# Values of one head and gates of the preceding head projected as one 512-column panel

## The chip, the core and the metric

The kernel runs on one core of a Trainium2 chip. The metric is the device time of one execution, in microseconds; lower is better. Engines are called by the names of the profile: PE is TensorE, ACT ScalarE, DVE VectorE, POOL GpSimd, SP SyncE (here a queue of DMA issues).

## The reference

One inference step of a layer with two groups of eight heads, for a prompt of 1024 tokens and for 8 x 16 = 128 sample tokens:

```
h = rms_norm(x, norm_pre)
q_sb, k_sb, v_sb, gate_sb, q_r, k_r, v_r, gate_r = split(h @ w_in)      # 8 kinds x 8 heads x 128
o_sb = stick_breaking(q_sb, k_sb, v_sb)        # per 128-query block, causal; samples over a cache of 1024
o_r  = retention(rope(q_r), rope(k_r), v_r)    # chunks of 64, a 128x128 state per head
y_sb = rms_norm_per_head(o_sb) * gain * silu(gate_sb)
y_r  = rms_norm_per_head(o_r)  * gain * silu(gate_r)
out  = concat(y_sb, y_r) @ w_out
x   += rms_norm(out, norm_post)
```

All is float32. The new keys and values and the retention states are outputs too.

## The kernel before

**Products.** A float32 product is done as three matmuls on float32r operands: high x high, high x low, low x high, where `split` (L165) makes the high part on ScalarE and the low part on VectorE. The tokens go in two groups: group 0 is four prompt tiles of 128 and the sample tile (640 tokens), group 1 the other four prompt tiles (512). The normalised tokens of a group lie in SBUF, transposed (model dimension on partitions), as high and low parts; the weights of `w_in` come from memory in blocks of 256 KB through tile `wr` (five buffers) and are split into `wh` and `wl` (four buffers). The 2048 rows of a weight are 16 k-tiles.

**Column panels** (`project`, L401; `products`, L382). For six of the eight kinds a panel is one head's 128 columns: the weights are the stationary operand, the tokens move, 256 + 384 columns in group 0, 512 in group 1. The result is transposed (head dimension on partitions, tokens along the row), which queries, keys and, before, gates need. One panel is 48 steps of k and term, each followed by a `tick` (L228). A panel uses one bank of tag `acc0` and, in group 0, one of `acc1`; there are two of each.

**Row panels** (`project_rows`, L424). Values are needed with tokens on partitions. Here the tokens are stationary, a tile of 128 at a time, and the weights of a pair of heads move, 256 columns. One panel serves heads h and h+1 of one kind; two token tiles share a bank. The values of retention are `rv`, those of attention `vn`. ScalarE copies them out with each token's inverse root (`root_of`).

**Gates** (`gate`, L475). A gate panel is a column panel; its result is scaled (VectorE), goes through a sigmoid (ScalarE) and is multiplied by it (VectorE): silu, transposed. The finish of a branch (`Out.finish`, L705) normalises the head's outputs (tokens on partitions), writes them to memory and reads them back in 32-blocks that a VectorE transpose completes (`turn_out`, `turn_in`: the "turn"), then multiplies gain, outputs and gate and stores the result to `s_y`, from which the output projection reads.

**Order.** The order is written by hand. The panels of a head come as query, key and gate of retention, then query and key of attention, the values of a pair at every second head, the gate of attention; retention's values of the next pair follow an odd head. Around the last heads the order differs (L1183 to L1196). The work of attention and retention lies between the matmuls of the panels: each is a generator (`Job`, L222) that yields a number of ticks to wait; `tick` advances the clock by one and runs one step of one job that is due. The constants `D_...` (L30 to L60) are these waits. `drain` (L241) ticks without products until a job is done: retention's job of the preceding head is drained behind the next head's query panel of retention, attention's job and the sample's `decode` behind the next query panel of attention. `tied` and `pin` keep some instructions from being placed ahead of the last product. What is written goes through a scheduler, which makes the order of each engine's queue from it.

Beside these jobs, in group 1, a job `sums` makes sums of blocks of `w_out` (40 items) for an output projection in seven products, and `residuals` writes the input rows to the outputs. Banks of PSUM: four for panels, two for score tiles (`score_tile`, L688; a third one in group 1), one each for `psa` and `psd`.

## Time and profile before

| | |
|---|---|
| time, median of 3 runs | 2277.81 us (2276.71 to 2277.94) |
| the profiled execution, first to last instruction | 2278.3 us |
| matmuls | 14306 |
| granted TensorE clock, mean | 0.996 |
| moved by DMA | 463.13 MB, mean 203 GB/s |

Busy times of engines overlap. A group's row gives line, engine, operation, output <- inputs, shape and count, then its busy time in us and the mean ns of one, then the idle time of the engine just before it and what ended most of it. The chain of work that ended last is followed back from the last instruction; in order of time it gives start, us and what. A row of waits gives in total, times, longest. A DMA issue gives count, KB each, median us to landing. Matmuls are pipelined, so the mean duration of one is longer than the distance from one to the next.

### The profile page before, as it was taken

To read this page: it belongs to the slowest core of one execution; us is meant where nothing else is said; L and a number is where in the kernel's file an instruction comes from. 1 tells how busy PE (TensorE), PEld (TensorE's weight loads), DVE (VectorE), ACT (ScalarE), POOL (GpSimd) and SP (SyncE) were. 2 spreads that over 40 slices of the span, in tenths; PEclk is the share of its full clock that TensorE was granted. 3 is DMA by queue.
4 is the path that set the end of the run, shared out by engine and by line. 5 is a ranking of instruction groups with operands and counts; after the bars stand their busy time and mean duration, and the time that the engine had idled before them with its cause. 6 is when DMAs were issued, how large, how long until landed. Compare 5 with 4: busy or idle time off the path is not lost.

```text
span 2278.3 us, 38962 instructions
## 1 busy us (share of the span) xinstructions
PE 2241.5 (98%) x14306; PEld 2023.3 (89%) x14306; DVE 1263.7 (55%) x2606; ACT 919.8 (40%) x1951; POOL 340.6 (15%) x577
## 2 busy tenths in 40 slices
PE   8999999999999999999999999999999999999998
PEld 8999999999999999999887989888888988788886
DVE  5435544454545454456556665766665667555567
ACT  6433333333333333335343334343343445435363
POOL 0012120301202030121111111120212212000020
PEclk9999999999999999999999999999999999999999
DMA  8747656675656657578778888878787758865596
GB/s 284 233 153 199 196 159 194 176 220 159 182 194 181 194 165 209 177 200 269 193 225 207 220 220 235 206 226 238 220 231 213 216 165 190 252 205 182 146 222 172
DMA packets 440832, 463.13 MB, mean 203 GB/s; under 512 B 182336, under 2 KB 302144, under 8 KB 440128
## 3 DMA queue, kind: packets, MB, share of 16 engines
q1 hardware_dynamic: 318400, 300.16, 46.5%
q0 software_dynamic: 28720, 78.41, 12.3%
q10 hardware_dynamic: 93520, 82.07, 11.4%
q8 instruction: 112, 1.84, 0.3%
q14 instruction: 80, 0.66, 0.1%
HBM read 359.58 MB, written 110.36 MB: 206 GB/s over the span
## 4 chain that ended last, share of the span: by engine, by line
PE 88%; DMA 5%; DVE 3%; issue 2%; ACT 2%; SPq 0%; POOL 0%; DVEq 0%; ACTq 0%; POOLq 0%
PE acc L387 46%; PE accn L446 17%; PE a L1213 5%; PE a L1214 5%; PE a L1210 5%; PE pa L783 3%; PE z L753 2%; PE pd L886 1%; PE zc L822 1%; DMA ro<-s_rk 1%; DMA s_rk<-rk 1%; PE pa L931 1%; PE pS L946 1%; DVE kp L682 1%; DMA wr<-w_cols 1%
## 5 line engine op out<-in xcount | busy, mean ns | idle before, releaser
L387 PE MATMUL acc<-mh,wh 128*128 128x256 f32 (+2 forms) x2304 | 667.4, 341 | 6.9 <-ACT wh L167 6.9
L387 PE MATMUL acc<-ml,wh 128*128 128x256 f32 (+2 forms) x2304 | 662.7, 340 | 0.2
L387 PE MATMUL acc<-mh,wl 128*128 128x256 f32 (+2 forms) x2304 | 659.8, 338 | 0.0
L168 DVE TENSOR_TENSOR wl<-wr,wh 128x512 fp32r<-128x512 f32 x504 | 345.9, 689 | 428.0 <-ACT wh L167 401.7
L167 ACT ACTIVATE wh<-wr 128x512 fp32r<-128x512 f32 x504 | 317.3, 631 | 641.2 <-PE acc L387 347.2
L387 PEld LDWEIGHTS acc<-mh,wh 128*128 128x128 f32 x2304 | 421.4, 189 | 39.2 <-ACT wh L167 6.9
L387 PEld LDWEIGHTS acc<-ml,wh 128*128 128x128 f32 x2304 | 422.9, 189 | 32.1 <-issue 3.3
L387 PEld LDWEIGHTS acc<-mh,wl 128*128 128x128 f32 x2304 | 425.5, 189 | 27.8 <-DVE wl L168 0.2
L446 PE MATMUL accn<-whn,mh 128*128 128x256 f32 x1152 | 328.1, 285 | 0.0
L446 PE MATMUL accn<-wln,mh 128*128 128x256 f32 x1152 | 325.8, 283 | 0.8 <-DVE wln L168 0.8
L446 PE MATMUL accn<-whn,ml 128*128 128x256 f32 x1152 | 325.7, 283 | 0.0
L446 PEld LDWEIGHTS accn<-whn,mh 128*128 128x128 f32 x1152 | 220.7, 192 | 2.7 <-issue 0.8
L446 PEld LDWEIGHTS accn<-wln,mh 128*128 128x128 f32 x1152 | 220.7, 192 | 1.8 <-DVE wln L168 1.0
L446 PEld LDWEIGHTS accn<-whn,ml 128*128 128x128 f32 x1152 | 220.7, 192 | 0.0
L167 ACT ACTIVATE whn<-wrn 128x512 fp32r<-128x512 f32 x128 | 80.5, 632 | 183.2 <-PE acc L387 74.2
L168 DVE TENSOR_TENSOR wln<-wrn,whn 128x512 fp32r<-128x512 f32 x128 | 87.6, 687 | 117.4 <-ACT whn L167 113.5
L646 POOL DMA_DIRECT2D be<-s_be x128 | 94.1, 741 | 149.5 <-DMA s_be<-be 126.4
L682 DVE TENSOR_TENSOR_SCAN kp<-kp 128x1152 f32<-128x1152 f32 (+4 forms) x40 | 82.7, 2067 | 45.7 <-POOL kp L671 29.1
L809 POOL DMA_DIRECT2D kcT<-cache_k x64 | 34.6, 545 | 442.2 <-PE pd L886 268.2
L1210 PE MATMUL a<-wh,mh 128*128 128x512 f32 x240 | 94.0, 392 | 1.8 <-ACT wh L167 1.8
L671 POOL TENSOR_SCALAR_AFFINE_SELECT kb<-kb 128x128 f32<-128x128 f32 x64 | 29.8, 474 | 433.2 <-ACT kb L665 430.9
L1213 PE MATMUL a<-wl,mh 128*128 128x512 f32 x240 | 94.3, 393 | 0.2 <-DVE wl L168 0.2
(272 smaller groups left out, 2968.7 us busy)
## 6 DMA issues: line engine op xcount, KB each, us to landing
wr<-w_cols SPq DMA_DIRECT2D x384, 256.0 KB, 4.4
wrn<-w_rows SPq DMA_DIRECT2D x128, 256.0 KB, 3.7
kcT<-cache_k POOLq DMA_DIRECT2D x64, 512.0 KB, 8.2
vc<-cache_v SPq DMA_DIRECT2D x64, 512.0 KB, 6.0
wr<-s_b SPq DMA_DIRECT2D x80, 256.0 KB, 4.1
br<-w_out SPq DMA_DIRECT2D x64, 256.0 KB, 4.9
s_b<-br ACTq DMA_DIRECT2D x32, 512.0 KB, 5.5
wr<-w_out SPq DMA_DIRECT2D x48, 256.0 KB, 3.7
```

The costliest lines, as they stand in the source:

```text
L167: nc.scalar.activation(hi, src, AF.Copy),
L168: nc.vector.tensor_tensor(lo, src, hi.bitcast(F32), ALU.subtract),
L387: last = nc.tensor.matmul(a[:, :m], lhs[:, j, :], rhs[w][:, j, o : o + m], start=(w == 0 and j == 0 and n == 0), stop=(w == KT // WQ - 1 a ...
L446: anchor[0] = nc.tensor.matmul(a, lhs[q][:, jj, ts], rhs[:, j, :], start=(w == 0 and j == 0 and n == 0 and t % 2 == 0), stop=(w == KT // 2 ...
L646: q.dma_start(raw[32 * i : 32 * i + 32, :].rearrange("p (k a) -> p k a", a=32), s[:, :, 32 * i : 32 * i + 32].rearrange("k (j b) a -> b (k ...
L682: nc.vector.tensor_tensor_scan(rev, rev, rev, 1.0, ALU.mult, ALU.bypass)
L753: nc.tensor.matmul(z[:, :c], q2[a][:, i * P : (i + 1) * P], k2[b][:, s : s + c], start=(m == 0), stop=(m == 2),)
L783: nc.tensor.matmul(po[:, :P], at[:, j, :], vn[:, j, :], start=(j == 0), stop=(j == t))
L809: ready.append((kc, nc.gpsimd.dma_start(kc, cache_k[h, m // 4, m % 4])))
L1210: ins = nc.tensor.matmul(a, hi[k][:, ts], wh, start=first, stop=False)
L1213: nc.tensor.matmul(a, hi[k][:, ts], wl, start=False, stop=False)
L1214: anchor[0] = nc.tensor.matmul(a, lo[k][:, ts], wh, start=False, stop=last)
```

## The change

The gates are made with tokens on partitions, like the values, and both kinds of gate of head h-1 share one panel with both kinds of value of head h: four blocks of 128 columns, so 512 columns move past each token tile. The first values panel and the last gates panel of each group have 256 columns. Queries and keys stay column panels. The first query panel of attention takes the place of the first gate panel in the opening.

The middle panel takes four accumulation banks, one for each token tile, and in group 0 a score bank for the fifth. It ticks twice for each token tile and k-tile, 0.75 each. At its end each tile is copied out (values) and goes through a sigmoid that reads PSUM with the token's inverse root as scale, and a fused multiply (gates). The finish multiplies outputs, inverse root and gate before the turn, a token tile at a time; behind the turn only the gain is left. A branch's finish waits until the gates of its head are there, which is behind the next head's middle panel.

Values are in a tile of two buffers, `vv`, by head and group; in group 1 the four old value tiles come back from memory into a tile of their own, `vo`, ahead of the job. The waits for values in attention fall away. The host lays the weights out for the new panels.

```
-COLS = (0, 1, 3, 4, 5, 7)
-ROWS = (2, 6)
+COLS = (0, 1, 4, 5)
...
-    def tick():
-        clock[0] += 1
+    def tick(by=1):
+        clock[0] += by
...
-    def project_rows(g, mov, col, dst, off, loads=None, roots_first=None):
+    def project_rows(g, mov, part, banks, out, loads=None, first=True, ready=None):
...
+        nt, width = len(g["tiles"]), part.shape[-1]
+        per = 512 // width
+        share = 1 if per == 2 else 0.75
+        for w in range(KT // per):
+            wr = wp.tile([P, per, width], F32, name="wrn", tag="wr", bufs=5)
+            nc.sync.dma_start(wr, part[:, per * w : per * (w + 1), :])
...
+            wh = wp.tile([P, per, width], F32R, name="whn", tag="wh")
+            wl = wp.tile([P, per, width], F32R, name="wln", tag="wl")
             split(wh, wl, wr)
-            for j in range(2):
+            for j in range(per):
+                k = per * w + j
                 for t in range(nt):
...
                     for n, (lhs, rhs) in enumerate(((hi, wh), (hi, wl), (lo, wh))):
                         anchor[0] = nc.tensor.matmul(
-                            a,
+                            banks[t],
                             lhs[q][:, jj, ts],
                             rhs[:, j, :],
...
                         )
-                    tick()
+                        if per == 1 and n == 1:
+                            tick(share)
+                    tick(share)
...
         for t in range(nt):
+            out(t, banks[t], root_of[:, tiles_before(g) + t : tiles_before(g) + t + 1])
...
-        def gate(acc, tag):
...
+        def value_rows(key):
+            values[key] = ep.tile([P, 5, 2, P], F32, name="vv", tag="vv", bufs=2)
+
+            def out(t, a, root):
+                nc.scalar.activation(values[key][:, t].rearrange("p j d -> p (j d)"), a, AF.Copy, scale=root)
+
+            return out
+
+        def gate_rows(key):
+            made = ep.tile([P, 5, 2, P], F32, name="gg", tag="gg")
+
+            def out(t, a, root):
+                s = ep.tile([P, 2 * P], F32, name="sg", tag="sg")
+                nc.scalar.activation(s, a, AF.Sigmoid, scale=root)
+                nc.vector.scalar_tensor_tensor(
+                    made[:, t].rearrange("p j d -> p (j d)"), a, root, s, ALU.mult, ALU.mult
+                )
+                gated[key] = made
+
+            return out
+
+        def first_values(g, mov, loads=None, ready=None):
+            project_rows(g, mov, w_val, half_banks(g), value_rows((phase[0], 0)), loads, True, ready)
+
+        def last_gates(g, mov, loads=None):
+            project_rows(g, mov, w_gate, half_banks(g), gate_rows((phase[0], H - 1)), loads, False)
+
+        def between(g, mov, h):
+            banks = [accp.tile([P, 512], F32, name=f"accm{t}", tag=f"acc{t % 2}") for t in range(4)]
+            if SAMPLE in g["tiles"]:
+                banks.append(score_tile("accm4"))
+            v, u = value_rows((phase[0], h)), gate_rows((phase[0], h - 1))
+
+            def out(t, a, root):
+                v(t, a[:, : 2 * P], root)
+                u(t, a[:, 2 * P :], root)
+
+            project_rows(g, mov, w_mid[h - 1], banks, out)
...
-            first = *first, pair["r"][:, :, 0, :], dict(rg=gate(project(g0, mov, col(7, 0)), "rg"))
+            first.append(project(g0, mov, col(0, 0)))
...
-            def finish(self, b, h, gT, oT, dst):
+            def finish(self, b, gi, h, at, oT, dst):
                 rs = inv_rms(op, self.ssq, P, "o")
-                nc.vector.tensor_tensor(
-                    self.o, self.o, rs.unsqueeze(2).to_broadcast([P, self.nt, P]), ALU.mult
-                )
+                for i in range(self.nt):
+                    nc.vector.scalar_tensor_tensor(
+                        self.o[:, i, :], self.o[:, i, :], rs[:, i : i + 1], gated[gi, h][:, at + i, b, :], ALU.mult, ALU.mult
+                    )
...
                 tied(nc.vector.transpose(oT[:, :n], flat))
-                nc.vector.scalar_tensor_tensor(
-                    gT[:, :n], oT[:, :n], gains[:, b, h : h + 1], gT[:, :n], ALU.mult, ALU.mult
-                )
-                nc.scalar.dma_start(dst, gT[:, : self.nt * P])
+                nc.vector.tensor_scalar(flat, oT[:, :n], gains[:, b, h : h + 1], None, ALU.mult)
+                nc.scalar.dma_start(dst, flat)
...
-            while "rg" not in rest:
+            while (gi, h) not in gated:
                 yield 3
-            yield from out.finish(1, h, rest["rg"], rk, s_y[gi][H + h])
+            yield from out.finish(1, gi, h, 0, rk, s_y[gi][H + h])
...
+                    if gi == 1:
+                        vo = ip.tile([P, 4, P], F32, name="vo", tag="vo", bufs=1)
+                        nc.sync.dma_start(vo, s_v[h])
+                        rest["vn"] = [vo[:, i, :] for i in range(4)] + new
                     sb_job = Job(sb_branch(gi, g, h, out, q2, k2, kT, rest), D_NAT[phase[0]])
...
                 if (gi, h) == (0, 0):
-                    order = ret_start, attention, gates
-                elif gi == 0 or h < H - 3:
-                    order = ret_queries, ret_keys, ret_gate, attention, gates
-                elif h == H - 3:
-                    order = ret_queries, ret_keys, attention, ret_gate, gates
+                    order = ret_start, attention
+                elif gi == 0 or h < H - 2:
+                    order = rows, ret_queries, ret_keys, attention
                 elif h == H - 2:
-                    order = ret_queries, attention, ret_keys, ret_gate, gates
+                    order = rows, ret_queries, attention, ret_keys
                 else:
-                    order = attention, ret_queries, ret_keys, ret_gate, gates
+                    order = rows, attention, ret_queries, ret_keys
...
+            after = [[], []]
+            loads = first_left() if gi else load_moving(after, 0, NB_TOK, from_h)
+            if gi == 0:
+                next(loads)
+            last_gates(g, mov, loads)
...
+        "w_val": beside(w[2, 0], w[6, 0]),
+        "w_mid": a(np.stack([beside(w[2, h], w[6, h], w[3, h - 1], w[7, h - 1]) for h in range(1, H)])),
+        "w_gate": beside(w[3, H - 1], w[7, H - 1]),
```

Here `rows` runs the middle panel of its head (`between`), or at the first head of group 1 the first values panel.

158 lines of the change are left out of this document (48 added, 110 removed).

## The prediction

> **What bounds the kernel now.** I read the page first: busy shares, the forty slices, the chain of work that ended last.
>
> ```profile
> span 2278.3 us, 38962 instructions
> PE 2241.5 (98%) x14306; PEld 2023.3 (89%) x14306; DVE 1263.7 (55%) x2606; ACT 919.8 (40%) x1951; POOL 340.6 (15%) x577
> ...
> PE   8999999999999999999999999999999999999998
> ...
> PE 88%; DMA 5%; DVE 3%; issue 2%; ACT 2%; SPq 0%; POOL 0%; DVEq 0%; ACTq 0%; POOLq 0%
> ```
>
> TensorE is busy in every slice and carries 88% of the chain. No other engine passes 55%. Then the waits of PE, to see what is not pure streaming:
>
> ```profile
> PE pa L783 <- DVE kp L743: 8.1, 7, 2.4
> PE acc L387 <- ACT wh L167: 6.9, 1, 6.9
> PE pb L557 <- DVE dg L555: 3.1, 1, 3.1
> ```
>
> These are the three largest, and only the first recurs. So the end moves almost one for one with what the stream of matmuls costs, and there is little idle time to win back. Now the groups of instructions with the shapes kept apart (count, then busy us and mean ns of one):
>
> ```profile
> L446 PE MATMUL accn<-whn,mh 128*128 128x256 f32 x1152 | 328.1, 285 | 0.0
> ...
> L387 PE MATMUL acc<-mh,wl 128*128 128x512 f32 x768 | 303.5, 395 | 0.0
> ...
> L387 PE MATMUL acc<-mh,wh 128*128 128x384 f32 x768 | 260.5, 339 | 0.0
> ...
> L387 PE MATMUL acc<-mh,wh 128*128 128x256 f32 x768 | 222.5, 290 | 6.9 <-ACT wh L167 6.9
> ...
> L1210 PE MATMUL a<-wh,mh 128*128 128x512 f32 x240 | 94.0, 392 | 1.8 <-ACT wh L167 1.8
> ```
>
> Each row is one of three like it (the three terms of the split product). The means include the pipeline's depth, so they overlap and cannot be added. What a matmul costs in a stream I take from unbroken stretches of the chain (start, us, count):
>
> ```profile
> 190.69 11.74 PE acc L387 x80
> ...
> 1360.20 12.72 PE acc L387 x56
> 1382.43 13.31 PE accn L446 x111
> ```
>
> 11.74/80 = 146.8 ns is the mean of a 256 and a 384 piece (group 0, column panels); 12.72/56 = 227.1 ns a 512 piece (group 1); 13.31/111 = 119.9 ns a 256-wide row matmul. Between 256 and 512 the slope is (227.1 - 119.9)/256 = 0.419 ns a column, which leaves 12.7 ns that each matmul pays whatever its width. That fixed part is what the change can save.
>
> **The change part by part.**
>
> *Matmuls.* Removed are the gate panels: 16 in group 0, each 48 pairs, so 1536 matmuls x 146.8 = 225.5 us; 16 in group 1 of 48, so 768 x 227.1 = 174.4 us; and all 3456 row matmuls x 119.9 = 414.4 us. Together 5760 matmuls, 814.3 us. Added are seven middle panels a group, 16 k x 3 terms x 5 or 4 token tiles: 1680 + 1344 = 3024 of 512 columns, and one values and one gates panel a group, 864 of 256 columns. 3024 x 227.1 + 864 x 119.9 = 686.8 + 103.6 = 790.4 us. The streamed columns are the same, the instructions 1872 fewer. Saving: **23.9 us**. The 227.1 is for weights stationary; the new form has tokens stationary and weights moving, which the L1210 row has too, at 392 against 395 ns, so I take the same price.
>
> [...]
>
> *Weight loads and splits.* The blocks stay 256 KB:
>
> ```profile
> wr<-w_cols SPq DMA_DIRECT2D x384, 256.0 KB, 4.4
> wrn<-w_rows SPq DMA_DIRECT2D x128, 256.0 KB, 3.7
> ```
>
> 384 + 128 = 512 before; after, 4 kinds x 16 panels x 4 = 256, 14 x 16 = 224, and 4 x 8 = 32, again 512, each with the same split. SP's queue gets the same number. The load of the old values in group 1 (vo) goes ahead of its head's work instead of behind its values panel; its one buffer was last read by the preceding head, which is drained earlier. Cost 0, hidden by five weight buffers; without that cover one landing, about 4 us, a head.
>
> *Scalar and vector work.*
>
> ```profile
> L458 ACT ACTIVATE rv<-accn,root_of 128x256 f32<-128x256 f32 x36 | 14.0, 475 | 13.1 <-PE accn L446 13.1
> ...
> L480 ACT ACTIVATE sw<-sg 128x256 f32<-128x256 f32 x8 | 3.3, 418 | 0.3 <-DVE sg L468 0.3
> ...
> L940 DVE SCALAR_TENSOR_TENSOR ro<-pa,dec,ro 128x128 f32<-128x128 f32 x56 | 19.4, 347 | 11.1 <-ACT ro L939 11.0
> ...
> L707 DVE TENSOR_TENSOR so<-so,or 128x512 f32<-128x512 f32 x16 | 11.0, 690 | 0.4
> ...
> L1015 DVE SCALAR_TENSOR_TENSOR st<-st,pSs 128x256 f32<-128x256 f32 x16 | 5.9, 412 | 1.0 <-PE pd L1011 0.8 <-PE accn L446 0.2
> ...
> L468 DVE TENSOR_TENSOR kT<-acc,roots 128x384 f32<-128x384 f32 x8 | 4.4, 548 | 0.0
> ```
>
> The gate of a token tile becomes one sigmoid (about 418 ns) and one fused multiply (412 ns). In finish, one 512-wide multiply of 690 ns becomes four 128-wide ones of about 347, 0.7 us later in a chain that ends in a DMA. Over the kernel VectorE and ScalarE stay within about 10 us of what they had, at 55% and 40%. On the end: 0.
>
> *New wait one: the middle panel takes all four accumulation banks.* At its start the third tile needs the bank of the key panel just ended, 2 tiles x 3 x 0.227 = 1.36 us after the first matmul. The key panel's evacuation is a 256- and a 384-wide multiply, the second 548 ns, ahead of a possible scan. A row panel of five tiles did the same before, re-taking its first bank after 12 x 0.12 = 1.44 us, and its groups show no more than 0.8 us of idle in all. Between 0 and 1 us a panel; I take 0. At its end the next query panel needs the first bank (in group 0 the second as well). Queued behind that wait on PE is every later product. The last matmul on tile 0 ends 12 x 0.227 = 2.7 us before the panel does (9 x 0.227 = 2.0 in group 1). A tile needs 475 + 418 on ScalarE and 412 on VectorE, so the first bank is free 1.4 us (0.7) early and the second 0.5 early. A split (632 ns) or a table load falling there uses that up:
>
> ```profile
> L167 ACT ACTIVATE whn<-wrn 128x512 fp32r<-128x512 f32 x128 | 80.5, 632 | 183.2 <-PE acc L387 74.2 <-PE accn L446 69.1 <-issue 15.9
> L183 ACT ACT_TABLE_LOAD x32 | 41.1, 1283 | 1.1 <-DVE ov L182 0.5
> ...
> L480 ACT ACT_TABLE_LOAD x9 | 11.5, 1283 | 3.4 <-DVE rg L468 3.3
> ```
>
> Both together make 0.632 + 1.283 - 0.5 = 1.4 us. Fourteen panels: 0 to 20 us. Nine of the 32 gate panels met a load before, so I take the low side, 0.3 us a panel, **+4 us**.
>
> *New wait two: in group 0 the fifth tile holds one of the two score banks through the panel* (about 54 us of each head). Score tiles then take turns in the other; each is held by two sigmoids or one multiply, while a job's next score tile is 9 ticks, some 4 us, away. 0 to 1.2 us for each collision; **+1 us**.
>
> *The clock of the jobs.* Steps of attention and retention are released by ticks. A group 0 head had 6 x 48 + 80 = 368 ticks; it now has 4 x 48 + 16 x 5 x 1.5 = 312, in as much time. Retention of a head needs 8 + 32 + 32 + 81 + 18 ticks, up to 80 waiting for scores, 15, and 64 for its finish, which now starts only behind the next middle panel, 48 + 48 + 120 = 216 ticks in. It is drained at 264, where at least 280 and up to 330 are needed (before: 320 there). So at seven heads some 16 to 66 ticks run with no product between, and what the other jobs have due is pulled in too. In group 1 a head has 288 ticks (352 before), and attention's 11 + 210 + 36 = 257 are drained at 240. The turns through memory that lose their cover take:
>
> ```profile
> s_bd<-be ACTq DMA_DIRECT2D x8, 576.0 KB, 9.9
> be<-s_bd SPq DMA_DIRECT2D x32, 144.0 KB, 3.1
> ...
> s_be<-kb POOLq DMA_DIRECT2D x8, 256.0 KB, 2.8
> kb<-s_be POOLq DMA_DIRECT2D x32, 64.0 KB, 5.7
> ```
>
> Whether PE waits depends on the order in its queue. That order is not the written one, as the timeline of ScalarE shows at the end of a key panel:
>
> ```profile
> 204.90 0.63 ACT L167 ACTIVATE wh<-wr 128x512 fp32r<-128x512 f32 x1 [1.03 <-PE acc L387]
> 205.56 0.38 ACT L488 ACTIVATE sw<-acc 64x256 f32<-64x256 f32 x1
> ```
>
> The rope's copy is written ahead of the next panel's splits and runs behind one. Work that is ready passes work that is not; so I expect the products to pass the late steps, and only errors of that order to cost. The bounds are 0 and one turn of 8.5 us at each of seven heads, 60 us; errors so far cost 8.1 us in seven places (first wait row). I take **+2 us**.
>
> The drain of the summed weights ahead of the last gates falls in the same class: 40 items of 58 ticks, 2320, from about tick 252 of group 1 reach 300 past its 2336 - 64; the drains themselves count about 24 ticks at each of eight heads, so some 110 ticks, two items, come in a burst. They are the last two, read near the end of the second product behind the gates, over 30 us later. 0.
>
> Sum: -23.9 + 4 + 1 + 2 = -16.9. On the profiled execution 2278.3 - 16.9 = 2261.4; the median of the runs is 0.5 us under its span, so **2261 us**. A measurement of this kernel can tell about 0.2%, 4.6 us, from no change.
>
> **The rivals.**
>
> *The new waits cost nothing, and old ones go.* With the re-spaced steps some of the 8.1 us at L783 vanish: 2278 - 24 - 4 = 2250. For it: the PE queue has ready products. Against: the steps are closer together than before, not farther. 0.07.
>
> *Slower: the drains make PE wait.* Place: the weighted sums of values (L783) and of the cache behind the drains of group 0. If half of the 8.5 us turn is exposed at each of seven heads, and again at seven of group 1, that is 14 x 4.25 = 60 us: 2278 - 24 + 60 = 2314; it decides from 1.7 us a head. For: the same kind of wait reached 2.4 us in the first row. Against: there it occurs seven times in all, and the order defers what is not ready. A mild form, 2 to 3 us a head, gives 2282 to 2296. 0.14.
>
> *The new form pays more.* If a 512-wide matmul with a new stationary operand each time paid the two-piece panel's rate, 293.6/640 = 0.459 ns a column, it would take 234.9 ns; 3024 x 7.8 = 23.6 us eat the saving, and with 7 us of waits the time is 2285. Against: the L1210 row. 0.04.
>
> *The bank waits eat most of it.* With 1.4 us at each of fourteen panels the gain is 23.9 - 20 - 3 = 1: 2277. For: the ends of the middle panel have only 0.5 to 1.4 us of cover. Against: half of the panels would need load and split both. 0.10.
>
> **How the numbers follow.** The forecast's own case, 7 to 24 us gained, has 0.65. Faster by over 0.2%: 0.65 + 0.07 and a little of the bank case, 0.74. Within 0.2%: most of the bank case and the mildest drains, 0.11. Slower: 0.15. The range goes from 2250 (every new wait free) to 2281 (bank waits in full, mild drains); its upper end stands in the slower cases, since the unknown costs reach there.
>
> **What would show it.** Right: 3024 new 512-wide matmuls in unbroken stretches at about 227 ns, 864 at 120, 12434 matmuls in all, PE's share still 97 to 98%, its waits up by a few us, some on the copies or gate multiplies of the middle panel. Wrong: stretches above 230 ns (the form), PE waiting more than 25 us in all for transposes (the drains), or for the release of banks (the panel's ends).

## The result, and the profile after

The changed kernel takes 2429.93 us (median of 4 runs, 2422.57 to 2434.33) against 2277.74 for the kernel before beside it: 1.0665 times as long, 95% interval 1.0646 to 1.0683. The forecast was 2261. It was wrong by 169 us and on the wrong side.

The page of the kernel after; a digit is the busy share of a fortieth of the span, in tenths:

```profile
span 2429.6 us, 35354 instructions
...
PE 2264.2 (93%) x12434; PEld 1946.1 (80%) x12434; DVE 1258.8 (52%) x2686; ACT 896.9 (37%) x1953; POOL 358.1 (15%) x577
...
PE   8997997979979799797999999999999997899998
...
PEclk9998998989989899898999999999999998999999
```

The matmuls are the 12434 that were counted, but PE falls from 98% to 93%, and in the first half of the span dents recur in PE's row and in the granted clock. To place them, the span is cut in three: up to the first 512-wide column matmul (group 0), up to the first matmul of the output projection (group 1), and the rest. Columns: us, busy us of each engine with its instructions, granted clock, DMA share, GB/s. Before:

```profile
0.00:1090.40 1090.40, 1077.23 (x8157) 1028.20 (x8158) 529.66 (x1172) 420.90 (x877) 169.09 (x317) 1.00 0.65 197
1090.40:1912.20 821.80, 810.34 (x4586) 702.71 (x4585) 510.87 (x961) 327.67 (x694) 148.83 (x234) 1.00 0.78 215
1912.20:2278.30 366.10, 353.92 (x1567) 292.43 (x1565) 223.14 (x474) 171.19 (x382) 22.67 (x28) 0.99 0.69 196
```

After:

```profile
0.00:1221.90 1221.90, 1098.07 (x6861) 973.35 (x6862) 527.44 (x1199) 392.56 (x861) 170.05 (x311) 0.94 0.58 176
1221.90:2057.50 835.60, 810.04 (x4010) 678.56 (x4008) 508.73 (x1006) 331.87 (x708) 165.15 (x238) 0.99 0.76 211
2057.50:2429.60 372.10, 356.04 (x1566) 294.22 (x1566) 222.64 (x482) 172.46 (x386) 22.86 (x28) 0.98 0.66 193
```

Of the 151.3 us between the two spans, 131.5 lie in group 0, 13.8 in group 1, 6.0 at the end. In group 0 PE's idle time (us less busy us) went from 13.2 to 123.8, which is 110.6; its busy time grew by 20.8 although the products there became shorter (1536 x 146.8 ns and 1920 x 119.9 ns gave way to 1680 x 227.1 and 480 x 119.9, 16.6 us less). So work that should have shrunk ran some 37 us slower, and the clock of 0.94 says why: half rate for some 12% of group 0. By the clock records of the trace that is 147 us; in 73.5 of them PE was busy, which costs it 36.8 us.

What PE waited for, whole span (us in total, times, longest):

```profile
PE acc L388 <- ACT wh L168: 85.6, 8, 13.4
PE pd L894 <- DMA vc<-cache_v: 15.8, 10, 3.5
PE pa L1018 <- DVE ro L1003: 14.4, 6, 2.7
PE pa L794 <- DVE kp L757: 9.9, 5, 4.8
```

The first row was 6.9 us, once, before, at the opening, and of the 85.6 us here 78 lie behind it, at seven places. It is no transpose and no bank: a column panel lacks its split weights. ScalarE makes them and is 37% busy, so the question is why the block was not there. (The third row, six places, is a bank: the products for the sample's new states wait until VectorE has read the bank `psa`. The kernel before has no such row.) One place of the first row, between heads 2 and 3, in the timeline of SP, ScalarE and PE (start, us, what, and in brackets the idle time before it and its releaser):

```profile
338.57 0.33 SPq L377 DMA_DIRECT2D wr<-w_cols  x1
...
340.61 5.14 SPq L661 DMA_DIRECT2D be<-s_bd  x2
353.50 1.95 SPq L661 DMA_DIRECT2D ro<-s_o  x4
355.50 2.18 SPq L661 DMA_DIRECT2D be<-s_bd  x2
357.85 0.98 SPq L860 DMA_DIRECT2D vc<-cache_v  x2
364.59 0.33 SPq L661 DMA_DIRECT2D so<-s_o  x1
371.68 0.80 SPq L860 DMA_DIRECT2D vc<-cache_v  x2
372.53 2.56 SPq L661 DMA_DIRECT2D so<-s_o  x3
375.19 11.89 SPq L661 DMA_DIRECT2D ro<-s_rk  x4
387.18 1.87 SPq L377 DMA_DIRECT2D wr<-w_cols  x4
...
390.63 0.63 ACT L168 ACTIVATE wh<-wr 128x512 fp32r<-128x512 f32 x1 [9.88 <-DMA wr<-w_cols]
...
391.31 0.90 PE L388 MATMUL acc<-mh,wh 128*128 128x256 f32 x2 [13.38 <-ACT wh L168]
```

SP issues one transfer after the other: of its 1324 issues in this trace no two overlap. Between the weight blocks at 338.57 and 387.18 lie 48.6 us in which it handles nothing but turn reads (`be`, `ro`, `so`) and cache loads, each waiting for its own write or its own sum. The program puts them next to each other: `drain` releases steps with no product written between, so no weight block comes between them on SP's queue either. What PE has in hand is five loaded and up to four split blocks of 4 k x 3 x 0.294 = 3.5 us of products each, by this estimate about 32 us, to which the jobs' matmuls in between add some; then it stands, here for 13.38 us. In group 0 such a stretch comes once a head, seven times. The seven longest, taken as the distances between SP's issues of weight blocks in group 0, are 44.1 to 48.6 us; in the kernel before none is over 13.6 (in both without one of some 17 us in the opening).

The last of the reads are slow as well: four of `ro<-s_rk` took 11.89 us, where four of the same form took 1.95 at 353.50. At 371 to 378 us the late cache sums freed eight buffers at once. The DMA issues from 370 to 392 us (KB each, median us to landing) have these:

```profile
kcT<-cache_k POOLq DMA_DIRECT2D x6, 512.0 KB, 8.1
vc<-cache_v SPq DMA_DIRECT2D x2, 512.0 KB, 4.5
```

And the same stretch in windows, columns as above:

```profile
379.00:387.00 8.00, 0.00 (x0) 0.00 (x0) 2.52 (x13) 0.69 (x4) 0.00 (x0) 0.56 1.09 327
387.00:391.00 4.00, 0.00 (x0) 0.00 (x0) 1.20 (x2) 0.37 (x1) 0.00 (x0) 0.50 0.86 222
391.00:400.00 9.00, 8.69 (x42) 8.69 (x43) 4.22 (x6) 2.78 (x5) 0.00 (x0) 0.67 0.68 208
```

Twelve microseconds without a matmul, the DMA engines at a share of 1.09 and then 0.86, the clock falling to 0.50; when PE starts again it is at 0.67 on average for 9 us.

### The profile page after: what moved, and what is told of

It reads as the page before. It is cut to its first block, busy times and chain, and to the rows that moved or that the text cites. A ratio compares the mean times of both kernels' runs of the same rounds, so it can differ in the third digit from the quotient of the medians.

```text
span 2429.6 us, 35354 instructions
## 1 busy us (share of the span) xinstructions
PE 2264.2 (93%) x12434; PEld 1946.1 (80%) x12434; DVE 1258.8 (52%) x2686; ACT 896.9 (37%) x1953; POOL 358.1 (15%) x577
## 5 line engine op out<-in xcount | busy, mean ns | idle before, releaser
L388 PE MATMUL acc<-mh,wh 128*128 128x256 f32 (+2 forms) x1536 | 459.7, 350 | 88.1 <-ACT wh L168 85.6
L388 PE MATMUL acc<-ml,wh 128*128 128x256 f32 (+2 forms) x1536 | 457.8, 349 | 0.0
L388 PE MATMUL acc<-mh,wl 128*128 128x256 f32 (+2 forms) x1536 | 452.9, 347 | 0.0
L432 PE MATMUL accm<-whn,mh 128*128 128x512 f32 x1008 | 394.8, 395 | 3.4 <-DVE kT L457 3.4
L432 PE MATMUL accm<-whn,ml 128*128 128x512 f32 x1008 | 396.3, 393 | 0.0
L432 PE MATMUL accm<-wln,mh 128*128 128x512 f32 x1008 | 394.2, 391 | 0.6 <-DVE wln L169 0.6
L388 PEld LDWEIGHTS acc<-mh,wl 128*128 128x128 f32 x1536 | 294.3, 196 | 20.2 <-issue 1.0
L432 PEld LDWEIGHTS accm<-whn,ml 128*128 128x128 f32 x1008 | 190.0, 188 | 44.9 <-issue 5.9
L432 PEld LDWEIGHTS accm<-whn,mh 128*128 128x128 f32 x1008 | 190.0, 189 | 40.5 <-DVE kT L457 4.3
L432 PEld LDWEIGHTS accm<-wln,mh 128*128 128x128 f32 x1008 | 190.1, 189 | 39.2 <-DVE wln L169 1.0
L686 POOL TENSOR_SCALAR_AFFINE_SELECT kb<-kb 128x128 f32<-128x128 f32 x64 | 32.3, 517 | 543.1 <-ACT kb L680 541.1
L697 DVE TENSOR_TENSOR_SCAN kp<-kp 128x1152 f32<-128x1152 f32 (+4 forms) x40 | 82.6, 2067 | 23.4 <-POOL kp L686 16.4
```

Of the source, the lines that this page charges most:

```text
L388: last = nc.tensor.matmul(a[:, :m], lhs[:, j, :], rhs[w][:, j, o : o + m], start=(w == 0 and j == 0 and n == 0), stop=(w == KT // WQ - 1 a ...
L432: anchor[0] = nc.tensor.matmul(banks[t], lhs[q][:, jj, ts], rhs[:, j, :], start=(k == 0 and n == 0 and (per == 1 or t % 2 == 0)), stop=(k ...
L686: nc.gpsimd.affine_select(blk, blk, pattern=[[-1, P]], base=0, channel_multiplier=1, compare_op=ALU.is_gt, fill=fill,)
L697: nc.vector.tensor_tensor_scan(rev, rev, rev, 1.0, ALU.mult, ALU.bypass)
```

## The experiments

Theory: the clock of the jobs, which is their count of ticks and not the granted clock of PE. A head of group 0 has 4 x 48 + 160 x 0.75 = 312 ticks where it had 368 (group 1: 288 where it had 352), in about as much time. Jobs are not done when the order wants them done, are drained, and their transfers stand in one row on SP ahead of the weights; PE idles and then runs at half its clock. Rivals: the five banks of the middle panel; the finish of retention, which must wait for the next head's gates; SP's order alone; the row panel itself.

The two columns after the ratio: us until group 0 ends, and the seven longest distances in it between SP's issues of weight blocks, without the one in the opening, which is 16 to 18 us in every run. The last: PE's wait for split weights (`acc <- ACT wh`) in all, of which one of some 7 us lies in the opening of every run.

| run | edit | us | ratio, 95% | group 0 | no weights | wait |
|---|---|---|---|---|---|---|
| | before | | | 1090.4 | 12.9 to 13.6 | 6.9 |
| | after | 2429.93 | 1.0665, 1.0646 to 1.0683 | 1221.9 | 44.1 to 48.6 | 85.6 |
| 1 | share 1.1 | 2333.46 | 1.0239, 1.0219 to 1.0259 | 1146.2 | 33.9 to 52.5 | 13.8 |
| 2 | turn reads on GpSimd | 2381.22 | 1.0458, 1.0423 to 1.0493 | 1144.4 | 11.4 to 19.4 | 6.8 |
| 3 | finish apart | 2348.97 | 1.0317, 1.0293 to 1.0341 | 1141.8 | 25.6 to 41.4 | 11.9 |
| 4 | late value-cache loads on GpSimd | 2390.26 | 1.0498, 1.0477 to 1.0519 | 1184.0 | 32.3 to 37.1 | 30.4 |
| 5 | kernel before, fewer ticks | 2359.71 | 1.0356, 1.0339 to 1.0372 | 1146.7 | 18.1 to 38.4 | 32.0 |
| 6 | 1.1, apart | 2317.92 | 1.0169, 1.0150 to 1.0189 | 1132.5 | 24.3 to 49.4 | 16.1 |
| 7 | 1.1, other bank | 2309.40 | 1.0137, 1.0116 to 1.0157 | 1120.3 | 27.8 to 32.3 | 9.4 |
| 8 | 1.1, states read early | 2389.11 | 1.0487, 1.0463 to 1.0510 | 1209.0 | 45.4 to 52.8 | 64.1 |
| 9 | 1.1, apart, other bank | 2298.44 | 1.0091, 1.0066 to 1.0115 | 1111.8 | 21.4 to 23.1 | 9.4 |
| 10 | run 9, sample part held back | 2286.23 | 1.0035, 1.0014 to 1.0056 | 1095.0 | 26.1 to 27.2 | 7.1 |
| 11 | 1.1, apart, held back | 2281.56 | 1.0011, 1.0000 to 1.0022 | 1094.9 | 26.8 to 27.8 | 6.8 |
| 12 | run 10 with 1.3 | 2321.02 | 1.0189, 1.0169 to 1.0209 | 1135.5 | 11.4 to 13.8 | 7.1 |
| 13 | run 11 with 0.75 | 2400.60 | 1.0542, 1.0520 to 1.0563 | 1192.6 | 34.3 to 46.8 | 18.7 |
| 14 | run 11, later turn reads | 2282.65 | 1.0022, 1.0007 to 1.0036 | 1089.8 | 26.7 to 28.0 | 6.6 |
| 15 | run 11, some turn reads on GpSimd | 2315.18 | 1.0166, 1.0148 to 1.0184 | 1117.8 | 26.8 to 27.5 | 7.4 |
| 16 | run 11 with 1.0 | 2323.97 | 1.0205, 1.0183 to 1.0227 | 1121.2 | 25.4 to 27.6 | 23.8 |
| 17 | run 11 with 1.15 | 2276.88 | 0.9993, 0.9981 to 1.0005 | 1089.3 | 20.5 to 21.7 | 7.2 |
| 18 | run 11 with 1.2 | 2276.45 | 0.9988, 0.9978 to 0.9998 | 1090.9 | 20.8 to 34.2 | 13.8 |

The ratio is to the kernel before on the same chip (2277.7 to 2279.6 us). Unless said, an edit is made to the changed kernel. "Share" is what one call of `tick` in a middle panel adds to the clock; 160 calls a head in group 0, 128 in group 1, so 1.1 gives 192 + 176 = 368 ticks in group 0, the old number, and 333 in group 1.

### The clock alone: runs 1 and 5

Run 1 lengthens the clock of the changed kernel, run 5 shortens that of the kernel before (to 304 and 288 ticks a head) and leaves its products as they were.

```
run 1:
-        share = 1 if per == 2 else 0.75
+        share = 1 if per == 2 else 1.1
run 5, in products and project of the kernel before:
-                tick()
+                if all_ticks or n == 2:
+                    tick()
...
-            products(mov, acc, g["pieces"], w, wh, wl)
+            products(mov, acc, g["pieces"], w, wh, wl, col[0] not in (3, 7))
```

> The changed kernel with one number altered: the middle panel ticks 1.1 instead of 0.75 twice for each k-tile and token tile, so that a head of group 0 has 192 + 176 = 368 ticks, as before the change. Theory (too few ticks: jobs are drained, turn reads stand close behind their turn writes on SP's queue, weight loads queue behind them): SP's waits of the turn reads (150 us in group 0 of the changed kernel, 16 before) fall under 40, PE's wait for the split of weights (85.6 us) under 15, time 2255 to 2290. Rival (the burst comes from the finish that now starts only behind the next middle panel, whatever the ticks): PE still waits 40 us or more for splits, time over 2340. Rival (the score bank held through the middle panel delays the jobs): time over 2380.

> The kernel before the change with one thing altered: its gate panels tick at one step in three, so that a head has 304 ticks in group 0 (368 before; 312 in the changed kernel) and 288 in group 1 (352; 288). Matmuls, banks and the place of the finish are those of before. Theory (the short clock alone makes most of the loss): SP's waits of the turn reads in group 0 go from 16 us to over 80, time 2340 to 2420. Rival (the loss needs the new panel: its held score bank, the finish behind it): time under 2310.

Run 1: 2333.46, 96 us below the changed kernel; the expected times of both sides were missed, since it lies between them; the theory's two signs came (SP's waits at the turn reads 31.7 us, PE's wait for splits 13.8), its time did not. Group 0 gets 76 us back, and what follows it takes as long as in the kernel before (2334.6 - 1146.2 = 1188.4 against 1187.9; 1207.7 in the changed kernel). Run 5: 2359.71, within the theory's range and 80 us above the kernel it was made from (2279.34 beside it), with not one matmul changed. PE's waits of run 1 and of run 5:

```profile
PE pa L794 <- DVE st L1022: 15.4, 6, 4.2
PE acc L388 <- ACT wh L168: 13.8, 8, 7.1
```

```profile
PE acc L387 <- ACT wh L167: 32.0, 6, 7.4
```

With the longer clock the wait for split weights goes from 85.6 to 13.8 us; with the shorter one it comes up in the old kernel, and its stretches without weights grow from 13 to 38 us. So the short clock is a cause on its own. That it is the largest holds only for one edit at a time, and not by far: the finish apart gives 81 us where the clock gives 96. What run 1 leaves, 55 us over the kernel before, is another matter; its first row, a wait for the state sums `st`, gave the next idea.

### What stands on SP's queue: runs 2 and 4

Run 2 moves the turn reads of the finishes and of the sample's decode to GpSimd's queue, so that no weight block stands behind them; run 4 moves the late loads of the value cache there.

```
run 2, both turns:
-                turn_in(s, flat, nc.sync)
+                turn_in(s, flat, nc.gpsimd)
run 4:
-                ld = nc.sync.dma_start(vc, cache_v[h, k])
+                ld = (nc.sync if k < V_BUFS else nc.gpsimd).dma_start(vc, cache_v[h, k])
```

> The changed kernel with its 0.75, but the reads of three turns (finish of retention, of attention and of the sample, and the sample's weights) are issued on GpSimd's queue instead of SP's. Theory in its strong form (SP blocked by the turn reads starves the split): PE's wait for splits falls from 85.6 to under 25 us and the time to 2300 to 2350, the rest being late cache sums and the slow clock behind them. Rival (the DMA engines are saturated by a burst of cache loads behind the late sums, and SP's order is of no matter): PE's wait stays over 60, time over 2390.

> The changed kernel with its 0.75, but the last two of a head's eight loads of cached values, which wait for a buffer that the first sums release, are issued on GpSimd's queue instead of SP's. Theory that SP stands still mainly at these loads (60 us in group 0, 81 before the change): PE's wait for splits under 40 us, time 2320 to 2370. Rival (the turn reads ahead of them have already delayed the sums, and the loads of weights meet the burst anyway): time 2400 to 2440, PE's wait over 60 us.

PE's waits in run 2, then in run 4:

```profile
PE pa L938 <- DVE sc L922: 17.5, 6, 4.6
...
PE accm L432 <- DVE kT L457: 12.9, 5, 4.0
...
PE acc L388 <- ACT wh L168: 6.8, 1, 6.8
```

```profile
PE pd L894 <- DMA vc<-cache_v: 32.3, 13, 4.9
```

Run 2 takes the wait for weights wholly away: the blocks did stand behind the turn reads, and the stretches without them fall to 19 us at most. Group 0 gets 77 us back. But the whole gains only 49 (56 between the two profiled executions), less than expected, since what follows group 0 grew from 1207.7 to 2373.4 - 1144.4 = 1229.0 us. From group 1 on the edit costs 21 us. And 54 us of group 0 stay: the steps are still due before their inputs, and PE waits for retention's decayed scores (`sc`) and the key panel's copies instead. Run 4 shortens the stretches to some 35 us and the wait for weights to 30.4, and pays a part back in late value caches; it gives 40, between the two ranges expected. SP's order is the way by which most of the short clock's cost in group 0 comes, and not all of its cost.

### The finish of retention apart: runs 3 and 6

The finish of retention waits for gates that the next head's middle panel makes; until then the whole job is not done, and `drain` ticks on. Here it becomes a job of its own.

```
-            yield from out.finish(1, gi, h, 0, rk, s_y[gi][H + h])
+            Job(out.finish(1, gi, h, 0, rk, s_y[gi][H + h]))
```

> The changed kernel with its 0.75, but the finish of retention is a job of its own, so that the drain behind the query panel does not include its 64 ticks. Theory that this one drain (some 60 ticks at each of seven heads) is the trigger: time 2270 to 2320, PE's wait for splits under 25 us. Rival (any head of 312 ticks is too short for the 341 of the sample's decode, so another drain takes its place): the next drain, that of the sample's job, shows, time 2340 to 2420.

> The changed kernel with both cures: 1.1 for 0.75, and the finish of retention a job of its own. Theory (what is left at 1.1, 56 us over before, is the drain of some 18 ticks behind the late finish): 2265 to 2300. Rival (what is left comes from the score bank that the fifth tile holds: the sample's state products need two score banks and the one of the sums): 2310 to 2335.

At 0.75 it gives 81 us, all in group 0, though the time of run 3 lies in the rival's range; at 1.1 it gives only 16 (2333.46 to 2317.92). Read the other way, the longer clock gives 96 us without this edit and 31 with it (2348.97 to 2317.92): the same lateness is cured by either, so they are not two causes to be added. In run 3 the wait for weights is down to 11.9 us and another has come up:

```profile
PE pa L938 <- DVE sc L922: 40.9, 7, 13.5
```

What is late there is the decay table `dT`: in the trace `sc` starts 0.4 to 0.6 us behind its landing, once 1.7, and its load stands on SP behind the turn reads. In run 6 the wait for `st` is still there with 15.0 us, as the rival had it.

### The score bank: runs 7 to 11

`st` is made of sixteen products a head that go to four banks, the two score banks, `psa` and `psd`. One score bank is what the middle panel of group 0 now holds for its fifth token tile. Run 7 puts that tile into the bank of tag `psd`, run 9 does so with the finish apart. Run 8 leaves the bank and lets the sample part of retention wait at most 8 ticks, not 80, for the decode's scores before it reads its states.

```
runs 7 and 9:
-                banks.append(score_tile("accm4"))
+                banks.append(psd.tile([P, 512], F32, name="accm4", tag="pd"))
run 8:
-N_READ = 40
+N_READ = 4
```

> The changed kernel with 1.1 for 0.75, and the fifth tile of the middle panel in the bank of the cache sums (psd) in place of a score bank. Theory of the score bank: the sample's state products are no longer cut in two, PE's waits of the attention sums for VectorE's states (15.4 us) go, time 2280 to 2315. Rival (the bank is of no matter, or psd is as badly missed as a score bank): 2320 to 2350.

> The changed kernel with 1.1 for 0.75, and retention's reading of the sample states waits up to 8 ticks for the decode's scores in place of up to 80. By a count of the yields the reading misses the first scores by some 10 ticks since retention has lost the 48 ticks of the gate panel as its head start, and waits some 97 ticks for the second. Theory that this delay is what is left: time 2270 to 2310. Rival (its products meet the held score bank in the middle panel either way): 2315 to 2345.

> The changed kernel with three cures: 1.1 for 0.75, retention's finish a job of its own, the fifth tile in the bank of the cache sums. If the three losses (clock, late finish, score bank) are separate, 2334 falls by 16 and by 24 to about 2294; if the finish and the bank are one loss, it stays at 2305 to 2312.

Run 7 gives 24 us, and the wait for `st` is gone. Run 9 agrees with bank and finish being separate: 24 and 16 off 2333.46 make 2294, measured 2298.44, within its interval; one loss under two names was to stay at 2305 or above. Run 8 went the other way, 56 us up, outside all that was expected:

```profile
PE acc L388 <- ACT wh L168: 64.1, 8, 9.6
```

The trace shows where the state products lie. In run 1 two of a head's sixteen run inside the middle panel and fourteen only behind it, 13 us later; in run 8 it is 31 us, since the first two come sooner and the panel's end does not (17 us in both at the first head). In run 7 twelve run inside the panel and only the four for `psd` wait for its end. In the changed kernel itself none falls into a panel: its short clock has all of them behind it. So this loss is one that only the longer clock brings up. That led to runs 10 and 11: a flag is up while a middle panel runs, and the sample part waits until it is down, then reads at once, without waiting for the decode's scores. Run 10 has the other bank, run 11 the score bank.

```
+            held[0] = True
             project_rows(g, mov, w_mid[h - 1], banks, out)
+            held[0] = False
...
-            if h:
-                waiting.append(read_states)
-                for _ in range(N_READ):
-                    if read:
-                        break
-                    yield 2
+            while held[0]:
+                yield 2
```

> As the kernel with the three cures, and the sample part of retention waits until no middle panel is under way, then reads the states at once; so its products never meet the held bank. Theory (what is left in group 0 are these products, cut off and put close behind the panel): 2255 to 2285, at best 24 us under the kernel before. Rival (what is left is the burst of loads behind the late cache sums, which this does not touch): 2290 to 2310.

> 1.1, retention's finish a job of its own, the sample part of retention outside the middle panels, but the fifth tile in a score bank as in the change. If the score bank hurts only through the products of the sample states: within 8 us of the same with the other bank. If it hurts the scores themselves too: 15 us or more over that.

Run 10: 2286.23; run 11: 2281.56, 36 us below run 6, which differs from it by this edit alone (that the wait for the decode's scores goes with it is not what helps: shortening it alone was run 8). So the held score bank hurts only through the sample's state products, and once these keep out of the panel the score bank is as good a place as the other. PE's largest waits in run 11 are the two that it had before: 7.5 us for `kp` and 6.8, once, for `wh`.

### How many ticks: runs 12, 13, 16, 17 and 18

With finish and sample part mended, only the share is changed. Do the ticks still matter?

```
-        share = 1 if per == 2 else 1.1
+        share = 1 if per == 2 else 0.75      (run 13; 1.0 run 16, 1.15 run 17, 1.2 run 18, 1.3 run 12)
```

> As the kernel with the sample part of retention held and the other bank, with 1.3 for 1.1: 400 ticks a head of group 0, 358 in group 1. If ticks are still short at 1.1 (sums of the cache late, loads in a burst), it gains 5 to 20 us; if 368 suffice, it stays within 5 us or is slower, the steps of a job then coming too close in time.

> Retention's finish a job of its own and the sample part of retention outside the middle panels, but the change's own 0.75 (312 ticks in group 0, 288 in group 1). Theory (each cure takes its own loss, the ticks the largest): 50 to 90 us over the same at 1.1, 2330 to 2370. Rival (the ticks hurt only because the sample part was drained; with that out of the way 312 suffice): within 20 us of 2282.

> At 1.0 in place of 1.1, with finish and sample part as above: 352 ticks in group 0. If the loss grows in steps with the missing ticks: 2285 to 2310. If 341 ticks of the decode are all that is needed: within 5 us of 2282.

> The kernel with 1.1 of a share, the retention's finish apart and the sample part held back (fifth tile in the score bank), with 1.15 of a share for the gate panel's ticks. The doses so far were 2400.6 us at 0.75, 2324.0 at 1.0 and 2281.6 at 1.1, and 2321.0 at 1.3 with the other bank. Theory that the best dose is the one at which a tick lasts equally long in every panel: one tick then stands for the same columns in the panel of gates as in the middle panels, which is near 1.17; so 1.15 gives 2262 to 2280 us, below the kernel before. Rival, that 1.1 was a lucky place for a few jobs and neighbouring doses move single waits about at random: 2282 to 2320.

> The same with 1.2 of a share. Theory of the equal tick: as near to 1.17 as the run beside it, 2262 to 2285 us. Rival: 2285 to 2325, towards the 2321.0 that 1.3 gave with the other bank.

0.75: 2400.6; 1.0: 2324.0; 1.1: 2281.6; 1.15: 2276.9; 1.2: 2276.5; 1.3 (other bank): 2321.0. With these two edits in, the ticks between 0.75 and 1.1 are worth 119 us, more than expected, and 1.0 too came out worse than both forecasts. It is no price of the ticks alone: at 0.75 the held sample part itself costs 52 us (run 13 against run 3), so a short clock and an edit that holds work back make each other worse. Run 13 shows the first mechanism again under another name. PE's first wait, and SP between heads 2 and 3:

```profile
PE pa L941 <- DVE sc L925: 70.9, 6, 13.0
```

```profile
367.87 9.79 SPq L664 DMA_DIRECT2D so<-s_o  x4
377.71 0.49 SPq L918 DMA_DIRECT2D dT<-c_dt  x1
378.29 1.80 SPq L377 DMA_DIRECT2D wr<-w_cols  x4
```

The turn reads keep SP for 9.79 us; behind them stand the decay table `dT`, without which VectorE cannot make `sc`, and then the weights. The wait row names VectorE, but what is late are transfers behind SP. Run 17 has the same reads with weight blocks between them:

```profile
316.35 3.94 SPq L664 DMA_DIRECT2D ro<-s_o  x4
327.05 0.83 SPq L863 DMA_DIRECT2D vc<-cache_v  x2
327.97 2.26 SPq L377 DMA_DIRECT2D wr<-w_cols  x2
338.10 1.92 SPq L664 DMA_DIRECT2D so<-s_o  x4
340.12 2.11 SPq L377 DMA_DIRECT2D wr<-w_cols  x4
```

Over the runs the two last columns of the table go together, but roughly: with distances of 44 us and more (after, run 8) PE waits 64 to 86 us for weights, with mostly 32 to 38 (runs 1, 4, 5) 14 to 32, and up to 32 hardly more than in the opening; run 18 has two distances of 34 us and two waits beyond the first, 7.0 us together. Run 16 does not fit (23.8 us with 27.6 at most), runs 1 and 5 differ by 18 us at much the same distances, and in runs 3 and 13 part of the wait is under `sc`.

At the long end, run 12 waits 34.1 us, 14 times, of column panels for the gate multiplies (`gg`) at a middle panel's end, at most 5.0 us at a time. That too many steps fall into the panel, so that its end is no longer clear, is likely and not shown.

A tick lasts 14.09 / 48 = 0.294 us in a column panel of group 0 (96 x 146.8 ns), and 240 x 0.227 / 160 = 0.340 per share of 1 in a middle panel; they are equal at a share of 1.16. The two doses beside it are the best, as forecast for that reason; but it holds for group 0 alone (the same sum for group 1 gives 1.5, which no run tried), and the flat stretch also covers the old number of ticks, 368. The runs do not tell the two reasons apart.

### Can the saving be had: runs 14 and 15

Run 11 still had SP waiting 63.6 us in group 0 for the write of attention's turn (`s_o<-so`). Run 14 puts 14 more ticks between that write and its read, run 15 moves the read to GpSimd.

```
run 14:
-                yield D_TO[phase[0]]
+                yield D_TO[phase[0]] + 14 * (b == gi == 0)
run 15:
-                turn_in(s, flat, nc.sync)
+                turn_in(s, flat, nc.sync if b else nc.gpsimd)
```

> At 1.1, with finish and sample part as above, and attention's finish in group 0 waits 46 instead of 32 ticks between the write and the read of its turn. SP waits 64 us in all for that write at seven heads, ahead of the weight loads. If this wait is where the rest of the saving of 23 us goes: 2262 to 2275, SP's wait under 15 us. Rival (five weight buffers cover 9 us; the rest goes in the matmuls of the jobs): 2277 to 2287.

> At 1.1, with finish and sample part as above, and the reads of attention's turns issued on GpSimd's queue, so that SP does not stand before them at all. Same theory as with the longer wait: 2262 to 2275; rival: 2277 to 2287, or more where GpSimd's own reads of the score turns come behind them.

Run 14: no difference (2282.65 against 2281.56), and the row is still at 60.2 us. Run 15: 34 us worse, with the row at 61.7. Neither edit took that wait away, and the trace says why: the row is `SPq L377 <- DMA s_o<-so`, a weight load that waits and not the turn read. By the semaphore numbers in the trace, this load signals on the same semaphore as the write (105 or 110) and is issued only when the write has landed; moving or delaying the read does not touch that. So the two runs did not test what they were made for. Run 17 has 61.9 us of waiting for the same write at the time of the kernel before, there at the turn read itself, so SP's waiting alone is not what is paid for. The best version stays run 18, 0.9988, with an interval that ends at 0.9998: some 2.6 us under the kernel before, which is within what counts here as no change. Its windows, cut as above:

```profile
0.00:1090.90 1090.90, 1071.59 (x6860) 945.71 (x6861) 525.39 (x1199) 385.84 (x859) 167.93 (x311) 1.00 0.65 197
1090.90:1900.00 809.10, 799.94 (x3982) 669.80 (x3981) 510.16 (x1000) 331.39 (x699) 156.14 (x235) 1.00 0.77 217
1900.00:2273.20 373.20, 357.29 (x1596) 295.45 (x1594) 224.10 (x488) 174.28 (x395) 25.36 (x32) 0.99 0.68 195
```

Groups 1 and end together are 5.6 us shorter, about the 7 that their products save. Group 0 is as long as before (1090.9 against 1090.4), though its products save 16.6. Counted from each matmul's start to the next in the trace of group 0, the distances behind jobs' matmuls sum to 134.9 us where they were 125.7, and what the products' own distances have beyond their plain price (117, 174.5 and 226.6 ns for 256, 384 and 512 columns, 119.9 for 256 of a row panel) sums to 40.2 where it was 33.0. That is 16.4 us, the whole saving of group 0, in many small waits. Some 3.4 us of it are half clock: by the clock records PE worked 10.2 us of group 0 at half rate where it was 3.4. No experiment removed the others one by one, so what makes them is open.

## Why the prediction was wrong, point by point

**The form of the matmuls: right.** The saving of 23.9 us stands. An unbroken stretch of run 18's chain has

```profile
256.11 12.48 PE accm L432 x55
```

12.48 / 55 = 226.9 ns with tokens stationary, against the forecast 227.1. This row decides: the rival "the new form pays more" falls, and the whole loss lies outside the products.

**The clock of the jobs, +2 us: this is the step that failed.** The prediction counted the ticks rightly (312 against 368, 288 against 352), saw that retention would be drained, and named bounds of 0 and 60. It then chose the low end because "work that is ready passes work that is not". That was read from ScalarE's queue. On SP's the transfers of a drained job came out next to each other, and whatever waits there holds all weight blocks behind it, for 44 to 49 us a head. The bounds were too narrow as well: they priced the turn that loses its cover (8.5 us at seven heads), where 78 us came up at the weight blocks behind the turns. And no term stood for what follows an idle stretch, half clock, to which the 37 us belong (36.8 by the clock records) by which PE's busy time in group 0 exceeds what its products should take. Measured, a shorter clock costs 80 us in the old kernel (run 5) and 96 in the new one (run 1), or 31 there if the finish is apart (run 6 against run 3).

**Weight loads at 0, "hidden by five weight buffers": failed with it.** The price without that cover, "one landing, about 4 us, a head", was too low: the blocks were not late by a landing, they were not issued for longer than all that PE had in hand, and a head lost up to 13.4 us.

**The finish behind the next middle panel.** The prediction saw the delay and put it under the drains. Alone it is 81 us (run 3), and 16 with the clock mended (run 6).

**The score bank, +1 us: not what made the loss.** I priced collisions of attention's score tiles, 9 ticks apart. What can collide are retention's sample state products, which the prediction did not look at. In the changed kernel they run behind the panel and do not meet its bank; with the old number of ticks they do, and cost 24 us by the other bank (run 7) and 36 by holding them back (run 11 against run 6).

**The bank waits at the panel's ends, +4 us: right in size at the start, little at the end.** The middle panel's matmuls wait 3.4 us in all for the key panel's copies (row L432 on the page after: `3.4 <-DVE kT L457 3.4`). At its end column panels wait for the gate multiplies for 11.9 us at a share of 1.0 (run 16) and 34.1 at 1.3 (run 12); at 0.75 (after, run 13) there is no such row.

**Scalar and vector work, 0: right.** VectorE 1258.8 us against 1263.7, ScalarE 896.9 against 919.8.

**The rivals.** The slower rival, drains that make PE wait, had the right cause, the wrong place (transposes at the weighted sums, which now wait 9.9 us against 8.1) and 60 us where it was 175 (151.3 longer, and 23.9 saved). What was to show the prediction wrong, PE waiting over 25 us for transposes or banks, did not come; PE waited for weights, which the list did not have.

**Not settled:** where most of the saving in group 0 goes when all three faults are mended, what a share of its own for group 1 would bring, and what the pulled-in sums of weights cost, which no run took apart.

## What to carry to other kernels

When work is released by counting instructions, an edit that changes their number or width changes a clock: keep the ticks per stage at the old number first, and only then ask what the edit is worth. For every wait that gets shorter cover, list what stands behind it on the same issuing queue, above all bulk loads that feed the bound engine; what to compare is the longest distance between two loads of the bound engine, here 44 to 49 us, and the work that its buffers hold, here some 32 us. The 1% saving in the stream (23.9 us) was lost here when the side work no longer arrived in time (the span grew by 151.3 us), so try the number of ticks as a dose of its own.

## What the runs showed of the hardware

The idle stretch of PE before 391.31 us is paid twice, the 13.38 us themselves and a slow clock behind them. In the windows around 391 us the granted clock stands at 0.50 and at 0.67 over the following 9 us, so PE ran at half rate for about 9 x (1 - 0.67) / 0.5 = 5.9 us. By the clock records of the trace the half rate goes on for 3.9 to 6.2 us behind the seven long stalls (8.9 to 13.4 us), 5.65 behind this one, and all half-rate stretches of group 0 are whole multiples of 3.41 us, from one to five. Such stretches come with shorter waits too. One of the six places where PE waits for `ro`, and the window behind it, columns as above:

```profile
486.28 0.55 PE L1018 MATMUL pa<-vv,rkn 32*128 32x128 f32 x1 [2.34 <-DVE ro L1003]
```

```profile
486.30:492.40 6.10, 6.10 (x29) 5.88 (x30) 2.50 (x6) 1.70 (x4) 2.58 (x4) 0.50 0.63 175
```

PE stood for 2.34 us and then ran for six at half rate. Of the 73.5 us of half-rate work in group 0, by the clock records, 34 follow the seven long stalls and 29 follow five of these six short waits. The timeline before and behind the long stall at 391 us:

```profile
373.71 0.56 PE L388 MATMUL acc<-mh,wl 128*128 128x256 f32 x2
374.11 0.46 PE L388 MATMUL acc<-mh,wh 128*128 128x256 f32 x2
374.41 0.46 PE L388 MATMUL acc<-ml,wh 128*128 128x256 f32 x2
...
392.01 0.74 PE L388 MATMUL acc<-ml,wh 128*128 128x256 f32 x2
392.54 0.74 PE L388 MATMUL acc<-mh,wl 128*128 128x256 f32 x2
```

A pair is 0.30 us from the next at full clock and 0.53 behind the stall. The first pair behind a job's matmuls takes 0.40. Over all such places in the first 1090 us at full clock the median is 381 ns against 293 for other pairs, before (129 places) and after (54) alike: each return from job work to products costs about 0.1 us here (88 ns).

The issue itself of small reads can be slow. Four turn reads took SP 1.95 us at 353.50 and 11.89 at 375.19, when the DMA engines stood at a share of 1.09 and 327 GB/s. Part of the first of the four may be a wait for VectorE, but the next two took 2.93 and 3.50 us with nothing in the trace that they waited for. In the first 1220 us of six of the traces, of 172 turn reads issued at a share under 0.5 (over 2.5 us) none took more than 1.83 us, and of some 380 at 0.8 to 1.2 the slowest took 8.02. So the issue itself, not only the landing, can be slow at a share of 0.8 to 1.2, and with it everything behind it on the queue; that the share is the reason is likely and not shown, since no run varied it alone, and most reads at a high share are quick.
